# Output projection, feed-forward tail, embedding gate and second block's first products by tiles of tokens, and the recurrent input turned two chunks earlier

## The chip, the cores and the metric

The kernel runs on one core of a Trainium2 chip, in one launch. The metric is the time of that core in microseconds (us); less is better. TensorE (PE) multiplies, VectorE (DVE), ScalarE (ACT) and GpSimd (POOL) work on what it needs and leaves, and SyncE (SP) issues most of the transfers.

## The reference, cut to what matters

The program is two transformer blocks over 256 tokens of 1024 features, in fp32. Only the parts that the change touches are shown; the mixers' inside is left out.

```python
# first block
merged = sigmoid(ga) * (y_a @ w_branch_a) + sigmoid(gb) * (y_b @ w_branch_b)
h = x + rms_norm(merged @ w_out, norm_post_mix)
v = rms_norm(h, norm_pre_mlp)
h = h + rms_norm(square(relu(v @ w_up)) @ w_down, norm_post_mlp)
h = h + rms_norm((p @ w_ple) * sigmoid(h @ w_ple_gate), norm_ple)
# second block
u2 = rms_norm(h, g_mix)
qa, ka, va, qb, kb, vb, qi, ki, wi, ga, gb = split(u2 @ w_in_2)
qa, ka = rope(qa), rope(ka)
...
x = x + hier_moe(...)   # 32 experts: 188 MB of weights, read at the program's end
```

## The kernel before

**Tiling.** The 256 tokens lie in two tiles `tt` of 128. `h` holds tokens on the partitions, while a product needs features there, so `h` is turned by PE transposes (`tps`) wherever it enters a product. Every fp32 operand is a pair, a rounded high part and a low part that is the rest, and every product is three passes (high by high, low by high, high by low). A weight matrix comes in chunks of 1 MB, 1024 rows by 256 columns. `wchunk` fetches one on SP's queue into `wraw` (3 buffers), then ACT casts it to `whi` in two halves (line 254) and DVE subtracts to give `wlo` in two halves (line 256), each with 2 buffers. A chunk is 48 matmuls of 256 columns. `fm` gives features on the partitions, both tiles of tokens in one matmul; `tm` and `tms` give tokens on the partitions, one tile after the other.

**Stages around the change.** In `mixer`, four chunks of `w_branch_b` on the attention's output (`mbb`), then the recurrent output `hg` is turned into `ya` (`tsplit`, 16 transposes) and four chunks of `w_branch_a` (`mba`) are multiplied with it and merged into `mh`. `w_out` (`mo`) takes two chunks for both tiles and the last two tile by tile. `PostNorm` then does, for each tile, a square with a running sum on ACT (`pm_j`, line 406), a multiply by the gain on DVE (`pm_fo`, line 407), a chain of nine small DVE operations for the inverse root (lines 198 to 214), and the update of `h` in two halves (line 414). `Turn.do(tt)` turns one tile of `h`: 8 transposes into two PSUM banks, and for each bank, if a gain goes in, a DVE multiply to `gx` (line 328), an ACT cast (line 329) and a DVE subtract (line 330), all of 128x512; without a gain an ACT cast and a DVE subtract (lines 362, 363). `products` are 48 matmuls on the embedding (`mple`) that depend on none of this. `feed_forward` goes over 16 chunks up (`mup`, relu squared on DVE, POOL, ACT, DVE into `hid`) and 16 down (`acc`, 512 columns, 24 matmuls a chunk); the last two chunks down go together, tile 0 first. Then PostNorm `pf`, the turn `pg`, the gate's product (`mpg`, four chunks in two pairs, each pair tile 0 then tile 1), PostNorm `pp`, the turn `u2`, and `block2`: `mmaq` in two chunks by tile, `mmak` in two chunks, ropes on DVE and POOL, transposes `px`, the index key `pxki`.

**What sets the order.** Each engine runs its instructions in one fixed order. A scheduler builds the order at compile time from the code's order, priorities and its own estimates, except where `tc.manual_schedule` pins PE to the code's order. `issue_after` keeps an instruction behind a named one on its engine. An operation early in an engine's order that still waits holds up all behind it.

Of the kernel before, what the change touches and what calls it, by code (L numbers as in the profile page):

```python
# [19 lines left out]
T = 256  # L20
# [12 lines left out]
T8 = 11  # L33
UNITS = 21
# [56 lines left out]
def tile_kernel(ctx: ExitStack, tc: tile.TileContext, a: dict, out: bass.AP, stages="1234", dbg=None):  # L91
# [92 lines left out]
    def rsqrt_steps(ss, dim, name, r, n=1, part=None):  # L184


        t = lambda k, dt=F32: small.tile([128, n], dt, name=name + k, tag="rn_" + k, bufs=4)
# [29 lines left out]
    def rsqrt_mean(ss, dim, name, out=None, n=1):  # L217
        r = out if out is not None else small.tile([128, n], F32, name=name + "r", tag="rn_r", bufs=4)
        run(rsqrt_steps(ss, dim, name, r, n))
        return r  # L220
# [16 lines left out]
    def wchunk(src, na, halves=False, after=None, act=None):  # L237
# [12 lines left out]
        hi = ws.tile([128, 2048], F32R, name="whi", tag="whi", bufs=2)  # L250
        lo = ws.tile([128, 2048], F32R, name="wlo", tag="wlo", bufs=2)
        for c in (slice(0, 1024), slice(1024, 2048)):
            with tc.issue_after(act) if act and c.start else ExitStack():
                cnt["hi"] = ACT.copy(hi[:, c], raw[:, c]).ins  # L254
            with tc.issue_after(after) if after else ExitStack():
                DVE.tensor_tensor(lo[:, c], raw[:, c], hi[:, c].bitcast(F32), op=OP.subtract)  # L256
# [91 lines left out]
    class Turn:  # L348
# [5 lines left out]
        def do(self, tt):  # L354
            hi, lo = self.u
            for k in (0, 4):
# [8 lines left out]
                self.end = scaled_split(hi[:, k:k + 4, c], lo[:, k:k + 4, c], ps, self.g[:, k:k + 4])  # L365

    def row_rstd(name, after=None):

        r = small.tile([128, 2], F32, name=name + "_r", tag="rr", bufs=4)
        for tt in range(2):  # L370
            ss = small.tile([128, 1], F32, name=name + "_ss", tag="rss", bufs=4)
            with tc.issue_after(after) if after and tt else ExitStack():
                ACT.activation(t8([128, D], name + "_j"), h[:, tt, :], AF.Square, accum_out=ss)
            rsqrt_mean(ss, D, name, r[:, tt:tt + 1])
        return r
# [151 lines left out]
    def embed():  # L527

        ptok = t8([128, 2, 256], "ptok")
        ACT.dma_start(ptok, a["p"][0, 0].rearrange("(c p) d -> p c d", p=128))  # L530
        px = t8([128, 2, T], "pxh", F32R), t8([128, 2, T], "pxl", F32R)
# [3 lines left out]
        def products():  # L535
            wp = wchunk(a["w_ple"][0].rearrange("(k p) c -> p k c", p=128), 2)
# [8 lines left out]
    def mixer():  # L545
# [384 lines left out]
        wb = a["w_branch_b"]  # L930
        for i in range(4):
            ps = mmt([128, 2, T], "mbb")
# [6 lines left out]
        ya = split2("ya")  # L939
        tsplit(hg, 8, *ya, g=gncol.to_broadcast([128, 8]))  # L940
        mh = split2("mh")
        for i in range(4):
            ps = mmt([128, 2, T], "mba")
# [849 lines left out]
```

## Time and profile before

| | us |
|---|---|
| median of 3 runs (lowest to highest) | 1313.97 (1312.89 to 1314.04) |
| the profiled execution's own time | 1311.6 |
| its span, first to last instruction | 1309.8 |
| PE busy | 1174.4 (90%) |
| DVE busy | 660.1 (50%) |
| ACT busy | 423.7 (32%) |
| POOL busy | 101.7 (8%) |

The profile is of one execution. Its time and its span differ by 1.8 us, which lie around the program. Where PE is busy in nearly every slice of a stage, each microsecond in which it stands still is a microsecond of that stage; late in the program the transfers of the experts' weights take all of the DMA engines. The views used further down are the page, tables of windows (busy time and count of instructions of each engine in a stretch, with PE's granted clock and the DMA share), the list of PE's waits, the rows of one engine in order of time, and groups of instructions by line.

### The profile page before, as it was taken

The page shows a single profiled execution, that of the slowest core. Times are in us where ns is not written, and L with a number is a line of the kernel's source. Part 1 is how long each engine was busy: PE and PEld are TensorE (multiplying, and loading weights), DVE is VectorE, ACT ScalarE, POOL GpSimd, SP SyncE. Part 2 cuts the span into 40 slices and gives each one's busy share as a digit, 9 for nine tenths or more (in the row PEclk, how much of TensorE's full clock was granted, in tenths as well). Part 3 has the DMA queues.
Part 4 walks back from the last instruction along what each step waited for, and adds up shares of the span by engine and source line. Part 5 has one row for each costly group of instructions (what it writes and reads, how often), then busy time and mean ns, then how long its engine had stood idle before and what let it go on. Part 6 is the DMA issues. An engine that isn't in the chain of part 4 may idle for free. (4 is left out here: it accounts for less than half of the span.)

```text
span 1309.8 us, 20713 instructions
## 1 busy us (share of the span) xinstructions
PE 1174.4 (90%) x8530; PEld 888.1 (68%) x8530; DVE 660.1 (50%) x1320; ACT 423.7 (32%) x799; POOL 101.7 (8%) x118
## 2 busy tenths in 40 slices
PE   7999999999998999998899999998969786877855
PEld 7898898999998999988798899963313222222211
DVE  6558876786667556657869776741101010101103
ACT  4455555244345434444444454420000000000001
POOL 0000000642001000010131011000000000000000
PEclk9999999999999999999899999999999899999998
DMA  8743433228564555564375474979999999999996
GB/s 265 258 132 103 129 108 118 66 66 189 172 205 136 186 179 184 191 201 152 91 236 173 160 265 163 368 296 426 427 426 428 427 426 427 426 427 427 427 423 236
DMA packets 145925, 332.15 MB, mean 254 GB/s; under 512 B 9169, under 2 KB 110498, under 8 KB 122274
## 3 DMA queue, kind: packets, MB, share of 16 engines
q1 hardware_dynamic: 140640, 327.18, 67.1%
q10 hardware_dynamic: 5186, 3.60, 1.0%
q8 instruction: 69, 1.13, 0.4%
q14 instruction: 30, 0.25, 0.1%
HBM read 329.70 MB, written 1.05 MB: 253 GB/s over the span
## 5 line engine op out<-in xcount | busy, mean ns | idle before, releaser
L256 DVE TENSOR_TENSOR wlo<-wraw,whi 128x1024 fp32r<-128x1024 f32 x226 | 292.7, 1314 | 107.4 <-ACT whi L254 107.4
L254 ACT CAST whi<-wraw 128x1024 fp32r<-128x1024 f32 x226 | 231.5, 1049 | 274.3 <-issue 64.7
L1518 PE MATMUL mh<-ew,xg 128*32 128x512 f32 x1024 | 184.9, 657 | 68.8 <-DMA ew<-in_w_dram 68.2
L1518 PEld LDWEIGHTS mh<-ew,xg 128*32 128x32 f32 x1024 | 42.4, 119 | 196.0 <-DMA ew<-in_w_dram 123.3
L1518 PE MATMUL ey<-ew,eth 128*32 128x512 f32 (+1 forms) x544 | 101.4, 572 | 14.9 <-DMA ew<-in_w_dram 14.3
L1518 PEld LDWEIGHTS ey<-ew,eth 128*32 128x32 f32 x544 | 26.8, 109 | 83.1 <-issue 40.8
L1000 PE MATMUL acc<-whi,hid 128*128 128x512 f32 x256 | 80.8, 395 | 0.7 <-DVE hid L989 0.7
L320 PE MATMUL mup<-v_hi,whi 128*128 128x256 f32 x256 | 72.5, 284 | 1.7 <-ACT v_hi L329 1.7
L320 PE MATMUL mgate<-u_hi,whi 128*128 128x256 f32 x256 | 73.2, 286 | 0.0
L1542 DVE SCALAR_TENSOR_TENSOR eth<-eth,gs,mh 128x512 f32<-128x512 f32 x8 | 6.0, 746 | 132.9 <-PE mh L1518 132.9
L320 PE MATMUL mup<-v_lo,whi 128*128 128x256 f32 x256 | 72.8, 284 | 0.1
L320 PE MATMUL mup<-v_hi,wlo 128*128 128x256 f32 x256 | 72.7, 284 | 0.0
L320 PE MATMUL mgate<-u_lo,whi 128*128 128x256 f32 x256 | 72.2, 282 | 0.0
L320 PE MATMUL mgate<-u_hi,wlo 128*128 128x256 f32 x256 | 72.1, 282 | 0.0
L1576 DVE TENSOR_TENSOR eyl<-ey,eyh 128x512 fp32r<-128x512 f32 (+1 forms) x17 | 11.1, 655 | 109.3 <-ACT eyh L1575 109.3
L1541 DVE SCALAR_TENSOR_TENSOR eth<-eth,mh 128x512 f32<-128x512 f32 x8 | 5.5, 687 | 104.2 <-ACT eth L1540 104.2
L1000 PEld LDWEIGHTS acc<-whi,hid 128*128 128x128 f32 x256 | 47.1, 188 | 12.1 <-DVE hid L989 1.5
L1548 ACT COPY eth<-ehT 128x512 f32<-128x512 f32 x8 | 4.7, 586 | 151.5 <-PE ehT L1547 151.5
L1000 PE MATMUL acc<-wlo,hid 128*128 128x512 f32 x128 | 50.9, 398 | 0.0
L320 PEld LDWEIGHTS mup<-v_hi,whi 128*128 128x128 f32 x256 | 48.9, 191 | 2.6 <-ACT v_hi L329 2.0
L320 PEld LDWEIGHTS mup<-v_lo,whi 128*128 128x128 f32 x256 | 49.0, 191 | 0.9 <-DVE v_lo L330 0.3
L320 PEld LDWEIGHTS mgate<-u_hi,whi 128*128 128x128 f32 x256 | 48.2, 188 | 1.6 <-issue 1.5
(661 smaller groups left out, 2833.3 us busy)
## 6 DMA issues: line engine op xcount, KB each, us to landing
ew<-in_w_dram SPq DMA_DIRECT2D x188, 1024.0 KB, 19.6
wraw<-in_w_in_dram SPq DMA_DIRECT2D x55, 1024.0 KB, 5.3
wraw<-in_w_up_dram SPq DMA_DIRECT2D x16, 1024.0 KB, 5.3
wraw<-in_w_down_dram SPq DMA_DIRECT2D x16, 1024.0 KB, 4.9
wraw<-in_w_out_dram SPq DMA_DIRECT2D x8, 1024.0 KB, 5.2
wraw<-in_w_branch_b_dram SPq DMA_DIRECT2D x16, 256.0 KB, 5.5
wraw<-in_w_branch_a_dram SPq DMA_DIRECT2D x4, 1024.0 KB, 5.1
wraw<-in_w_ple_gate_dram SPq DMA_DIRECT2D x4, 1024.0 KB, 5.2
```

The costliest lines, as they stand in the source:

```text
L254: cnt["hi"] = ACT.copy(hi[:, c], raw[:, c]).ins
L256: DVE.tensor_tensor(lo[:, c], raw[:, c], hi[:, c].bitcast(F32), op=OP.subtract)
L320: PE.matmul(ps[:, f, :], lhsT=w[v][:, k, c0 + f * 128:c0 + f * 128 + 128], rhs=x[u][:, k, :], start=k == 0 and i == 0, stop=k == nk - 1 an ...
L1000: PE.matmul(acc[tt][c], lhsT=x[:, p_, k, tt * 128:tt * 128 + 128], rhs=w[q_][:, k, c * 512:c * 512 + 512], start=j == 0 and k == 0 and i = ...
L1518: PE.matmul(ps[r, :], lhsT=lhsT[:, r], rhs=w[i][:, k, c], start=start, stop=stop)
L1541: DVE.scalar_tensor_tensor(hT, hT, 1.0, h1, op0=OP.add, op1=OP.mult)
L1542: DVE.scalar_tensor_tensor(hT, hT, gs, h3, op0=OP.mult, op1=OP.mult)
L1548: ACT.copy(hT, tp)
L1576: DVE.tensor_tensor(y[1], yp, y[0].bitcast(F32), op=OP.subtract)
```

## The change

- **Recurrent input.** `ya` is turned after the second of the four `mbb` chunks, with PE pinned to the code's order from there to the end of the first `up`. The last `mba` chunk is multiplied and merged in two halves.
- **Output projection.** The four `w_out` chunks are all kept, and tile 0 goes through all four (`quarter`: 24 matmuls of one tile and one chunk), then tile 1. The turn of tile 0 stands before tile 1's last quarter. `PostNorm` takes two pieces of 512 columns.
- **`Turn.do` with a gain.** Instead of three operations of 128x512 a bank, four slices of 128x128, each an ACT operation that scales and rounds from PSUM and a DVE operation that scales, subtracts and writes the low part. This holds for all turns with a gain: `u` at the start, `v`, and `u2`.
- **Feed-forward's tail.** Chunk 13 down moves behind chunks 14 and 15: tile 0 takes 13, 14, 15, then tile 1 takes 14, 15, 13, with the turn `pg` of tile 0 between 15 and 13.
- **Gate and second block.** The gate goes by quarters: tile 0 chunks 0 to 2, turn of tile 1, tile 0 chunk 3, tile 1 chunks 0 to 2, turn `u2` of tile 0, tile 1 chunk 3. `mmaq` and `mmak` become four chunks `mmaqk` in the same way, and the four ropes follow.
- **Weights.** `fifo` keeps the casts and subtracts of these chunks in issue order, and `room` puts some of them in extra buffers (`xhi`, `xlo`). `row_rstd` does both tiles in one chain.

SP's order of transfers, and the count of matmuls of each product, are the same in both.

```diff
@@ wchunk
+        hi = room([128, 2048], "xhi", F32R) if room else ws.tile([128, 2048], F32R, name="whi", tag="whi", bufs=2)
+        lo = room([128, 2048], "xlo", F32R) if room else ws.tile([128, 2048], F32R, name="wlo", tag="wlo", bufs=2)
         for c in (slice(0, 1024), slice(1024, 2048)):
-            with tc.issue_after(act) if act and c.start else ExitStack():
+            with tc.issue_after(cnt["hi"] if fifo else act) if fifo or act and c.start else ExitStack():
                 cnt["hi"] = ACT.copy(hi[:, c], raw[:, c]).ins
+            after = cnt["lo"] if fifo else after
...
@@ Turn.do
-                self.end = scaled_split(hi[:, k:k + 4, c], lo[:, k:k + 4, c], ps, self.g[:, k:k + 4])
+                for j in range(4):
+                    g = self.g[:, k + j:k + j + 1]
+                    cnt["split"] = ACT.activation(hi[:, k + j, c], ps[:, j, :], AF.Copy, scale=g).ins
+                    self.end = DVE.scalar_tensor_tensor(lo[:, k + j, c], ps[:, j, :], g, hi[:, k + j, c].bitcast(F32),
+                                                        op0=OP.mult, op1=OP.subtract).ins
@@ mixer
+        order = tc.manual_schedule(engines={PE.engine})
+        order.__enter__()
+        ya = split2("ya")
         for i in range(4):
+            if i == 2:
+                tsplit(hg, 8, *ya, g=gncol.to_broadcast([128, 8]))
...
+            w = wchunk(wcols(a["w_branch_a"][0], i * 256), 8)
+            for lo, hi in ((0, 2),) if i < 3 else ((0, 1), (1, 2)):
+                ps = mmt([128, hi - lo, T], "mba")
+                fm(ps, w, ya, c0=lo * 128, nf=hi - lo)
+                merge(ps, sga, sgb, mh, slice(2 * i + lo, 2 * i + hi))
...
+        w = [wchunk(wcols(a["w_out"][0], i * 256), 8, fifo=True, room=t8 if i in (0, 3) else None)
+             for i in range(4)]
         for tt in range(2):
+            for i in range(4):
+                if i % 2 == 0:
+                    ps = mmt([128, 2, 256], "mo")
+                if tt and i == 3:
+                    turn.do(0)
+                quarter(ps[:, i % 2, :], w[i], mh, tt)
+                if i % 2:
+                    pn.piece(i // 2, tt, ps.rearrange("p z c -> p (z c)"), 512)
+            pn.finish(tt, 2)
+    def quarter(ps, w, x, tt):
+        for k in range(8):
+            for i, (u, v) in enumerate(PASSES):
+                PE.matmul(ps, lhsT=x[u][:, k, tt * 128:tt * 128 + 128], rhs=w[v][:, k, :],
+                          start=k == 0 and i == 0, stop=k == 7 and i == 2)
@@ feed_forward
+        for j, w_ in tail:
+            down(0, j, w_, hid[j], last=j == 15)
+        finish(0)
+        w += [gate_w(i) for i in (1, 2)]
+        for j, w_ in tail[1:] + tail[:1]:
+            if j == 13:
+                turn.do(0)
+            down(1, j, w_, hid[j], last=j == 13)
+        finish(1)
...
+        for i in range(3):
+            gated(0, i)
+        turn.do(1)
+        w.append(gate_w(3))
+        gated(0, 3)
+        for i in range(4):
+            if i == 3:
+                then.do(0)
+            gated(1, i)
@@ block2
-        qw = [(mmt([128, 2, T], "mmaq"), wchunk(wcols(w_in, i * 256), 8, after=turn.end, act=cnt["split"] if i else None)) for i in range(2)]
-        tms(qw, u, mid=lambda: turn.do(1))
+        for i in range(3):
+            w.append(qk_w(i))
+            quarter(ps[i][:, 0], w[i], u, 0)
+        turn.do(1)
+        w.append(qk_w(3))
+        quarter(ps[3][:, 0], w[3], u, 0)
+        for i in range(4):
+            quarter(ps[i][:, 1], w[i], u, 1)
```

**Tail of the feed-forward, DVE.** `wlo` are the low parts of the gate's first two chunks, `pg_lo` the low part of the turned `h`, `pf_fo` and the `pf` operations PostNorm's. Before, from the update of tile 0 to the update of tile 1:

```order
L414 SCALAR_TENSOR_TENSOR h_76<-pf_fo_6280,pfr_6292,h_76 128x512 x2
L407 TENSOR_TENSOR pf_fo_6280<-acc10_4714,pf_g_6278 128x512
L363 TENSOR_TENSOR pg_lo_6283<-tps_6308,pg_hi_6282 128x4x128
L363 TENSOR_TENSOR pg_lo_6283<-tps_6315,pg_hi_6282 128x4x128
L407 TENSOR_TENSOR pf_fo_6280<-acc11_4715,pf_g_6278 128x512
L411 TENSOR_REDUCE pf_s2_6328<-pf_ss_6281 128x1
L256 TENSOR_TENSOR wlo_6355<-wraw_6352,whi_6354 128x1024
L198 TENSOR_SCALAR pfb_6331<-pf_s2_6328 128x1
L256 TENSOR_TENSOR wlo_6355<-wraw_6352,whi_6354 128x1024
```

In the changed kernel, from the update of tile 0:

```order
L419 SCALAR_TENSOR_TENSOR h_76<-pf_fo_6217,pfr_6267,h_76 128x512 x2
L259 TENSOR_TENSOR wlo_6286<-wraw_6283,whi_6285 128x1024 x2
L259 TENSOR_TENSOR wlo_6294<-wraw_6291,whi_6293 128x1024 x2
L366 TENSOR_TENSOR pg_lo_6220<-tps_6323,pg_hi_6219 128x4x128
L366 TENSOR_TENSOR pg_lo_6220<-tps_6330,pg_hi_6219 128x4x128
L412 TENSOR_TENSOR pf_fo_6217<-acc10_4734,pf_g_6215 128x512
L412 TENSOR_TENSOR pf_fo_6217<-acc11_4735,pf_g_6215 128x512
L416 TENSOR_REDUCE pf_s2_6355<-pf_ss_6218 128x1
L199 TENSOR_SCALAR pfb_6358<-pf_s2_6355 128x1
```

The four subtracts of the gate's weights now stand together between the first update of `h` and `pg_lo`, and no longer inside the chain of the second tile (before, two more followed there).

**Turn of `u2` for tile 0, ACT.** `pth` is the gate's tanh, `pp_j` PostNorm's square, and the casts are of the second block's first chunks. Before:

```order
L1027 ACTIVATE pth_6646<-mpg1_6491 128x512
L329 CAST u2_hi_4692<-gx_6633 128x4x128
L329 CAST u2_hi_4692<-gx_6642 128x4x128
L406 ACTIVATE pp_j_6649,pp_ss_6349<-pth_6646 128x512
L254 CAST whi_6715<-wraw_6713 128x1024
L373 ACTIVATE u2_j_6837,u2_ss_6836<-h_76 128x1024
L114 DMA cst2_6701<-in_cst_dram 128x384
L329 CAST u2_hi_4692<-gx_6774 128x4x128
L329 CAST u2_hi_4692<-gx_6783 128x4x128
```

In the changed kernel:

```order
L370 ACTIVATE u2_hi_4704<-tps_6607,colv_86 128x128
L256 CAST xhi_6720<-wraw_6718 128x1024
L370 ACTIVATE u2_hi_4704<-tps_6607,colv_86 128x128
L370 ACTIVATE u2_hi_4704<-tps_6620,colv_86 128x128
L256 CAST xhi_6720<-wraw_6718 128x1024
L256 CAST whi_6752<-wraw_6750 128x1024
L370 ACTIVATE u2_hi_4704<-tps_6607,colv_86 128x128
L370 ACTIVATE u2_hi_4704<-tps_6620,colv_86 128x128
L1069 ACTIVATE pth_6657<-mpg_6582 128x512
L256 CAST whi_6752<-wraw_6750 128x1024
L370 ACTIVATE u2_hi_4704<-tps_6607,colv_86 128x128
L370 ACTIVATE u2_hi_4704<-tps_6620,colv_86 128x128
```

The two casts of the turn have become eight slices; casts of the next weights, the last tanh and the last square stand between them.

**Second tile of the output projection, DVE.** `v_lo` are slices of tile 0's turn, `wlo_4740` the first `up` chunk. Before:

```order
L330 TENSOR_TENSOR v_lo_4567<-gx_4594,v_hi_4566 128x4x128
L330 TENSOR_TENSOR v_lo_4567<-gx_4603,v_hi_4566 128x4x128
L407 TENSOR_TENSOR pm_fo_4312<-mo1_4453,pm_g_4310 128x512
L411 TENSOR_REDUCE pm_s2_4610<-pm_ss_4313 128x1
L256 TENSOR_TENSOR wlo_4720<-wraw_4717,whi_4719 128x1024
L198 TENSOR_SCALAR pmb_4613<-pm_s2_4610 128x1
```

In the changed kernel:

```order
L412 TENSOR_TENSOR pm_fo_4323<-mo_4544,pm_g_4321 128x512
L371 SCALAR_TENSOR_TENSOR v_lo_4337<-tps_4569,colv_86,v_hi_4336 128x128
L416 TENSOR_REDUCE pm_s2_4622<-pm_ss_4324 128x1
L259 TENSOR_TENSOR wlo_4740<-wraw_4737,whi_4739 128x1024
L371 SCALAR_TENSOR_TENSOR v_lo_4337<-tps_4582,colv_86,v_hi_4336 128x128
L199 TENSOR_SCALAR pmb_4625<-pm_s2_4622 128x1
L259 TENSOR_TENSOR wlo_4740<-wraw_4737,whi_4739 128x1024
L371 SCALAR_TENSOR_TENSOR v_lo_4337<-tps_4582,colv_86,v_hi_4336 128x128
```

The second tile's chain had one subtract between `pm_fo` and `pmb`. Now it has a slice and a subtract before `pmb` and a slice, a subtract and a slice more behind it.

## Rows read from the trace of the kernel before

**Rows 1.** Page: span, engines with share and count, granted clock in 40 slices.

```profile
span 1309.8 us, 20713 instructions
...
PE 1174.4 (90%) x8530; PEld 888.1 (68%) x8530; DVE 660.1 (50%) x1320; ACT 423.7 (32%) x799; POOL 101.7 (8%) x118
...
PEclk9999999999999999999899999999999899999998
```

**Rows 2.** Windows at the end: length, each engine busy (count), clock, DMA share, GB/s.

```profile
860.00:870.00 10.00, 8.79 (x74) 5.34 (x74) 5.01 (x30) 2.30 (x8) 0.00 (x0) 1.00 0.37 131
870.00:880.00 10.00, 10.00 (x93) 5.18 (x94) 1.23 (x4) 0.64 (x2) 0.00 (x0) 1.00 0.99 407
880.00:1300.00 420.00, 328.33 (x1813) 107.61 (x1806) 55.23 (x108) 24.51 (x51) 0.00 (x0) 0.96 1.00 419
```

**Rows 3.** Windows of PE alone: length, busy (count), clock, DMA share, GB/s.

```profile
344.00:354.00 10.00, 8.86 (x69) 1.00 0.33 107
400.00:415.00 15.00, 11.24 (x75) 0.89 0.54 184
593.00:610.00 17.00, 13.38 (x91) 0.90 0.48 155
610.00:622.00 12.00, 12.00 (x102) 1.00 0.57 175
622.00:642.00 20.00, 15.24 (x100) 0.83 0.31 89
656.00:670.00 14.00, 12.05 (x101) 1.00 0.86 290
```

**Rows 4.** Windows of all engines, two at a low granted clock.

```profile
410.00:415.00 5.00, 5.00 (x32) 5.00 (x32) 2.49 (x10) 0.00 (x0) 0.00 (x0) 0.66 0.52 163
630.00:635.00 5.00, 5.00 (x23) 5.00 (x24) 5.00 (x16) 0.00 (x0) 0.00 (x0) 0.50 0.53 163
```

**Rows 5.** PE waits from 342 to 670: sum in us, times, longest.

```profile
PE mmaq L309 <- ACT u_hi L329: 2.2, 2, 1.2
PE mpg L309 <- DVE pfb L198: 2.0, 1, 2.0
PE mmaq L309 <- DVE ppb L198: 1.9, 1, 1.9
PE mup L320 <- ACT v_hi L329: 1.7, 1, 1.7
PE tps L359 <- DVE h L414: 1.6, 1, 1.6
PE pxki L1117 <- POOL ki L488: 1.4, 1, 1.4
...
PE acc L1000 <- DVE hid L989: 0.7, 2, 0.5
```

**Rows 6.** DVE in time, feed-forward tail: start, length, operation.

```profile
591.89 1.42 DVE L414 SCALAR_TENSOR_TENSOR h<-pf_fo,pfr,h 128x512 f32<-128x512 f32 x2
...
596.58 1.22 DVE L256 TENSOR_TENSOR wlo<-wraw,whi 128x1024 fp32r<-128x1024 f32 x1
...
597.77 1.22 DVE L256 TENSOR_TENSOR wlo<-wraw,whi 128x1024 fp32r<-128x1024 f32 x1
```

**Rows 7.** ACT in time, the same place.

```profile
588.72 0.60 ACT L406 ACTIVATE pf_j<-acc 128x512 f32<-128x512 f32 x1 [0.48 <-PE acc L1000]
```

**Rows 8.** ACT groups by line: count, busy, mean ns of one.

```profile
L254 ACT CAST whi<-wraw 128x1024 fp32r<-128x1024 f32 x226 | 231.5, 1049 | 274.3 <-issue 64.7 <-PE mup L320 60.9 <-PE acc L1000 40.3
...
L449 ACT ACTIVATE ats_p<-ats_s,ats_mx 128x128 f32<-128x128 f32 x16 | 6.0, 373 | 17.1 <-PE atw_pt L465 8.5 <-DVE ats_mx L447 8.5
```

**Rows 9.** DVE group by line and shape: count, busy, mean ns.

```profile
L1135 DVE SCALAR_TENSOR_TENSOR score<-rl,wi,score 128x128 f32<-128x128 f32 x8 | 2.7, 343 | 0.0
```

**Rows 10.** PE in time, program start, with the wait before.

```profile
11.76 0.58 PE L309 MATMUL mkv<-wlo,u_hi 128*128 128x256 f32 x1 [1.39 <-DVE wlo L256]
```

**Rows 11.** POOL in time, one rope of the second block.

```profile
660.97 2.12 POOL L488 TENSOR_TENSOR tokmak<-rope2z,rope2w 128x512 f32<-128x512 f32 x1 [4.48 <-DVE rope2z L486]
```

More of the change, by code (lines that the diff above doesn't have):

```diff
@@ L184, in rsqrt_steps @@
     def rsqrt_steps(ss, dim, name, r, n=1, part=None):
[L187 removed]
+        t = lambda k, dt=F32: small.tile([128, n], dt, name=name + k, tag=f"rn{n}" + k, bufs=3 if n == 1 else 1)
         b, sh, y, q, y2 = t("b"), t("s", I32), t("y"), t("q"), t("z")
@@ L217, in rsqrt_mean @@
     def rsqrt_mean(ss, dim, name, out=None, n=1):
-        r = out if out is not None else small.tile([128, n], F32, name=name + "r", tag="rn_r", bufs=4)
+        r = out if out is not None else small.tile([128, n], F32, name=name + "r", tag="rn1r", bufs=4)
         run(rsqrt_steps(ss, dim, name, r, n))
@@ L968, in merge, with feed_forward @@
         DVE.tensor_tensor(mh[1][:, c], sga[:, c], mh[0][:, c].bitcast(F32), op=OP.subtract)
-    def feed_forward(pw, turn, then):
+    def feed_forward(pw, turn, then, order):
         turn.do(1)
@@ L980, in up @@
             ps = mmt([128, 2, T], "mup")
-            fm(ps, wchunk(wcols(a["w_up"][0], j * 256), 8), v)
+            fm(ps, wchunk(wcols(a["w_up"][0], j * 256), 8, fifo=j == 0, after=turn.end if j == 1 else None), v)
             if j == 0:
@@ L986, in up @@
             POOL.tensor_tensor(r, r, r, op=OP.mult)
-            x = t8([128, 2, 2, T], "hid", F32R)
+            if j % 2 == 0:
+                hid["room"] = t8([128, 2, 2, 2, T], "hid", F32R)
+            x = hid["room"][:, j % 2]
             ACT.copy(x[:, 0], r)
@@ L1043, in block2 @@
         u = turn.u
-        qw = [(mmt([128, 2, T], "mmaq"), wchunk(wcols(w_in, i * 256), 8, after=turn.end, act=cnt["split"] if i else None)) for i in range(2)]
-        tms(qw, u, mid=lambda: turn.do(1))
+        ps = [(mmt if i < 3 else pt)([128, 2, T], "mmaqk") for i in range(4)]
+        w = []
+        qk_w = lambda i: wchunk(wcols(w_in, i * 256), 8, fifo=True, room=t8 if i in (0, 3) else None)
+        for i in range(3):
[6 more added lines that the diff above has]
+            quarter(ps[i][:, 1], w[i], u, 1)
+        order.__exit__(None, None, None)
+        qw, kw = ps[:2], ps[2:]
         r = row_rstd("u2", after=cnt["split"])
@@ L1726, in tile_kernel @@
     if "1" in stages:
-        pw, turn = mixer()
+        pw, turn, order = mixer()
     else:
```

128 lines of the change are left out of this document (60 added, 68 removed).

## The prediction

> **What bounds the kernel now.** I read the page first. PE is busy for 90% of the span [rows 1], so the question is where it stands still and whether the end would follow if it didn't. The windows late in the program answer the second part: from 880 us to 1300 us the DMA engines are full (share 1.00, 419 GB/s), while in the ten microseconds up to 870 their share is 0.37 [rows 2]. The end is 420 us of transfers of expert weights that start once the computation ahead of them has released buffers. So time saved on PE before 870 us should move the start of that block, and with it the end, one for one. Time saved inside the block would be worth nothing, but the change touches nothing there.
>
> Next I read the windows of PE alone around the places of the change. A stretch in which PE runs full gives the measure: 102 matmuls in the 12 us from 610 [rows 3], 0.118 us each (matmuls of 256 columns; those of 512, as in the products down, count twice). Against that measure:
> - 344 to 354, the turn of the recurrent output: 69 matmuls are 8.1 us of work, so 1.9 are lost.
> - 400 to 415, end of the output projection and first product up: 75 are 8.8, so 6.2 are lost.
> - 593 to 610, turn for the gate: 91 are 10.7, so 6.3 are lost.
> - 622 to 642, turn for the second block: 100 are 11.8, so 8.2 are lost.
> - 656 to 670, ropes and index key: 101 are 11.9, so 2.1 are lost [rows 3].
>
> Together 24.7 us: that is the ceiling for these places. Seven items of the list of waits name 11.5 us of it [rows 5]. A good part of the rest is the clock: from 630 to 635 the granted clock is 0.50, which is 1.2 GHz instead of 2.4, and 23 matmuls fit where 42 would, a loss of 2.2 us; from 410 to 415 it is 0.66, 32 matmuls, a loss of 1.2 us [rows 4]. Both spells begin right behind a place where PE stood still.
>
> **The change part by part.** Prices used throughout: a cast of half a chunk on ACT 1.05 us [rows 8], a subtract of half a chunk on DVE 1.2 us [rows 6]. The trace has no slice of the new turn. The nearest rows are an ACT operation of 128x128 with a per-partition operand, 0.37 us [rows 8], and a DVE operation of the same kind and size, 0.34 us [rows 9]. The order of the changed kernel lets the ACT slice of a bank wait for the DVE slice before it in that bank, so I take 0.71 us for each of a bank's four steps, 2.9 us a turn. Bounds: 0.37 if the two overlap, 1.3 if a slice cost what operations four times as long do (0.60 on ACT and 0.71 on DVE for 128x512 [rows 6, 7]).
>
> The Trainium skill, page PSUM — Partial Sum Buffer, section "PSUM bank collisions raise a hardware error", says that ACT and DVE must not be in one bank at once and that the compiler therefore makes one wait for the other, reads included. This rule speaks against cutting a bank into slices. No row of before shows it. Without it the turn would go at ACT's 0.37 us a step, and the term of the output projection below would be better by about 1 us.
>
> *Start.* The first pass on a low part waits 1.39 us for a subtract [rows 10]. The turn at the start also goes by slices, so DVE no longer does two whole multiplies and two whole subtracts ahead of it. Gain 0.8, between -0.3 (the slices hold up the casts of the weights) and 1.3 (all of the wait).
>
> *Recurrent input.* The transposes, casts and subtracts of `ya` now lie under 96 matmuls of the last two `mbb` chunks, 11.3 us of PE. DVE has four subtracts (4.8 us), two products and the turn (about 5.5 us) in them, so they fit, just. The wait for `ya` goes. Gain 1.8 of the 1.9, between 1.0 and 1.9.
>
> *Output projection.* Tile 0's chain and turn now lie under tile 1's quarters (24 matmuls, 2.8 us each), and cost nothing. Tile 1's don't: behind the last `mo` matmul, PE has 48 matmuls of the embedding, 5.65 us. The chain then needs the square, which stands behind casts on ACT (0.75 late, then 0.8 with its read), two subtracts and three slices that the order puts inside it (2.4 + 1.0), the small operations (1.25) and the update (1.4): 7.6 us. So PE still waits about 1.9 us at the transposes, where it waits 1.6 now [rows 5]. Then the first product up takes slices as they come: first low part after 0.71, the next only 1.05 us later still, because the square of the next norm stands on ACT between the first two slices; then one each 0.71 against 0.35 us of matmuls. That is 2.5 us of waiting, against 1.7 for the wait at that place now [rows 5]. Half speed behind it again, more likely than not: 0.7 of 1.2. Together 5.1 us lost, where 6.2 are lost now, and 0.2 more (of the 0.7 for `hid` [rows 5]) at the first product down. Gain 1.3, between -0.5 and 3.5.
>
> *Feed-forward's tail.* Tile 0's chain takes 4.6 us from the square of its last piece (588.72) to the end of the update (593.31) [rows 6, 7]. Now 24 matmuls of 512 columns of tile 1 lie over it, 5.6 us. The transposes then need not wait. Then come 12 matmuls of chunk 13, 2.8 us, and 0.9 of transposes. DVE does four subtracts (4.8 us) and the first `pg_lo` (0.7) after the update, 5.5 us, so `mpg` waits for about 0.6. I add 0.6 for the third gate chunk's weights, and 0.4 for small things. Tile 1's chain lies under 72 matmuls (8.5 us) and is free. The stop of 2.0 us for a subtract [rows 5], which stands in the order between the chain's operations, goes, and with it the half speed. Loss 1.6 instead of 6.8 (6.3, and ahead of the window 0.5, the longest wait for `hid` [rows 5]). Gain 5.2, between 3.5 and 6.5.
>
> *Gate to second block.* Tile 0's chain is covered by 72 matmuls in the same way. But the turn `u2` has only 24 matmuls, 2.8 us, over it, and on ACT casts stand between its slices. Counted from the end of the transposes along the order: five slices and three casts take 4.7 us, the tanh 0.6, a cast 1.0, so the fourth slice of the first bank is done at 6.6 and PE needs it at 3.9; a square and another cast stand before the last slice, done at 9.1. Ideally the first quarter ends at 5.6; by this it ends at 9.8. So 4.2 us lost, or about 1.5 if the casts run earlier than this order lets me see, and 0.4 for a chance of half speed behind it. Tile 1's chain and turn lie under the quarters and are free. Loss 4.4 instead of 8.2. Gain 3.8, between 0.5 and 6.5.
>
> *Ropes.* Four ropes of 2.1 us each on POOL [rows 11] now come one behind the other after one norm of both tiles, where they were spread over the products; the last transposes wait for them. Loss 0.4, between -1.0 (a gain, from the doubled chain) and 1.5. The wait for the index key, 1.4 [rows 5], stays. SP's transfers keep their order.
>
> Sum: 0.8 + 1.8 + 1.3 + 5.2 + 3.8 - 0.4 = 12.5 us. The profiled execution took 1311.6 us, 2.4 less than the median of 1313.97. Taken off the profile that gives 1299.1, off the median 1301.5.
>
> **The rivals.** *All cover holds.* If the slices overlap and casts don't stand in their way, the output projection loses 2.5 and the second block 1.5, and no half speed is left: 12.5 + 2.6 + 2.9, and the upper ends of start and tail (0.5 + 1.3), make 20 us, 1294. For it: PE has matmuls enough that don't depend on the turns. Against it: the order itself, in which ACT waits at slices with casts queued behind.
>
> *The waits come back.* ACT and DVE are in order, and every slice that waits holds casts, and every cast a product. If the second block's loss stays at 8 and the output projection's at 6.7, only the start, the recurrent input and 4 us of the tail are left, less 0.4: 6 us, 1308. For it: the wait of 2.0 us at the gate [rows 5] was of just this kind, a subtract behind a small operation that waited. Against it: 7 us of that loss are waits and clock which the quarters cover by counts.
>
> *Slower.* One mechanism: each step from ACT to DVE and back in one bank costs more than the two operations. Four turns lie open or nearly so (both at the start, the second `v`, the first `u2`), 16 steps; at 0.8 us more a step, 1.5 instead of 0.71, the gain is gone, and at 1.8, 1.1 more, the kernel is at 1319. Against it: now the chain from the square to the update, with its handings over, takes 4.6 us in all [rows 6, 7].
>
> *The end does not follow.* If the transfers of the expert weights were paced by something that the change doesn't move, the windows up to 870 us would show less waiting and the time would stay at 1313. For it: SP's order is unchanged. Against it: the share of 0.37 just before the block [rows 2]; the transfers wait for the computation there, not the other way round.
>
> **How the numbers follow.** Forecast of 1301.5, 0.58; all cover holds 0.14; the waits come back 0.17; the end does not follow 0.06; slower 0.05. A measurement of this kernel can tell about 0.2%, 2.6 us, from no change. Faster by more: the first three, less a little of the third, 0.87. Within: 0.09. Slower: 0.04. The range reaches from the first rival's 1294 to a little beyond the second's 1308, 1293.5 to 1309, with about 0.2 left out: the two last cases and tails of the first.
>
> **What the changed kernel's profile would show.** Right: no wait of PE at `mba`; transposes of `pg` and of tile 0's `v` without one; granted clock near full around the gate; waits left at the second `v` turn (1.9, then 2.5) and at the first `mmaqk` for `u2` (about 4); the DMA block beginning near 867 instead of 880. Wrong: a low granted clock at three places as before; waits for `xlo` or `wlo` in the gate's quarters of over 1 us; waits at `hid` or at the extra buffers, which share their room with it; a DMA block that begins no earlier.

## The result, and the profile after

The changed kernel takes 1296.09 us (median; 1293.66 to 1296.35) where the kernel before took 1313.43 beside it: 17.3 us less, ratio 0.9865 (95% interval 0.9847 to 0.9882). On another chip it took 1295.90 against 1312.33, 16.4 us less, ratio 0.9875 (0.9860 to 0.9890). The forecast was 12.5 us less, 1301.5 in a range of 1293.5 to 1309.0.

The page of the changed kernel, its span, engines and granted clock, beside [rows 1]:

```profile
span 1294.3 us, 20749 instructions
...
PE 1172.1 (91%) x8530; PEld 883.9 (68%) x8530; DVE 658.2 (51%) x1327; ACT 429.7 (33%) x832; POOL 100.0 (8%) x118
...
PEclk9999999999999999999999999999989899999988
```

The span is 15.5 us shorter and PE's busy time 2.3: most of the gain is time in which PE stood idle before. The medians differ by 1.8 us more than the spans, since the profiled execution of before (1311.6) was that much faster than the median of its runs, while the one of after (1296.05) was at its median.

Windows of PE alone at the places of the change (length, busy with count, clock, DMA share, GB/s), to be held against [rows 3]:

```profile
344.00:354.00 10.00, 10.00 (x87) 1.00 0.75 242
398.00:413.00 15.00, 13.38 (x99) 1.00 0.43 142
594.00:610.00 16.00, 15.62 (x131) 1.00 0.33 105
614.00:630.00 16.00, 14.35 (x101) 0.89 0.72 221
640.00:656.00 16.00, 14.05 (x118) 1.00 0.60 187
```

At 0.118 us a matmul, nothing is lost where `ya` is turned (87 matmuls in 10 us, 69 before), 3.3 us in the 15 us around the first product up (99, and 75 before), 0.5 us over the gate, 4.1 us in 614 to 630, the turn of `u2`, and 2.1 us in 640 to 656, the ropes. PE's waits between 330 and 657 us (sum, times, longest), beside [rows 5]:

```profile
PE pxki L1179 <- POOL ki L493: 1.5, 1, 1.5
PE tps L362 <- DVE h L419: 1.3, 1, 1.3
PE mmaqk L979 <- ACT u_hi L370: 1.0, 1, 1.0
PE mmaqk L979 <- DVE u_lo L371: 0.5, 1, 0.5
```

The stops at `mba`, and the long ones for a subtract at the gate (2.0 us) and in the second block (1.9), have gone. What is left of 1 us or more is the wait for the update at `tps`, the one for the slices of `u2`, and the one for the index key (1.4 before). The end followed: in the window below the DMA engines are full, and by windows of 2 us they are nearly so (0.94) from 855 us on, where before they were (0.90) from 870 on.

```profile
857.00:867.00 10.00, 10.00 (x93) 5.87 (x86) 1.47 (x3) 0.60 (x1) 0.00 (x0) 1.00 1.02 427
```

From the views by tile I read where the first or last matmul of each product starts, and so how much earlier than before each stage ends. Each column is the gain of one stretch in us (negative is a loss); each kernel's are of its one profiled execution.

| kernel | start to first `mbb` | to first `mo` | to first `acc` | to last `mpg` | to `pxki` | to the last matmul |
|---|---|---|---|---|---|---|
| the changed kernel | -0.10 | 2.37 | 2.33 | 4.76 | 5.89 | 0.31 |
| x12_changed_again (the same) | 0.19 | 2.37 | 2.40 | 4.74 | 5.53 | -0.54 |
| x9_u2_chain_first | 0.74 | 2.37 | 2.41 | 4.76 | 8.80 | 0.39 |
| x10_tail_by_chunks | -1.73 | 2.11 | 2.42 | -2.95 | 6.02 | 0.12 |
| x11_all_first | 0.68 | 2.11 | 4.09 | 4.76 | 8.82 | 0.36 |
| x6_u2_slices_first | 1.81 | 2.12 | 2.35 | 5.38 | 7.30 | -0.42 |
| x7_v_and_u2_first | 0.87 | 2.37 | 2.90 | 4.61 | 5.80 | -1.40 |
| x1_whole_turns | -3.14 | 1.99 | 2.85 | 5.50 | 5.04 | -0.50 |
| x2_ya_alone | -2.28 | 2.12 | -0.23 | 0.17 | -0.22 | -0.16 |
| x3_out_by_chunks | 1.15 | 2.12 | 1.75 | 5.25 | 6.01 | 0.48 |
| x4_tail_gate_by_chunks | 0.62 | 2.38 | 2.40 | -0.11 | 1.45 | 0.11 |
| x5_qk_by_chunks | 1.89 | 2.38 | 2.30 | 5.38 | 2.41 | 0.49 |
| x8_first_turn_cut | -0.36 | -0.22 | -0.71 | 0.0 | 0.0 | 0.18 |

In the changed kernel the eight transposes of the first `u2` lie ahead of the last `mpg` and no longer behind it (0.87 us), so by equal work tail and gate gained 5.6 and the second block 5.0. After `pxki` the gain stays as it is to the end.

### The profile page after: what moved, and what is told of

It reads as the page before. It is cut to its first block, busy times and chain, and to the rows that moved or that the text cites. A ratio compares the mean times of both kernels' runs of the same rounds, so it can differ in the third digit from the quotient of the medians.

```text
span 1294.3 us, 20749 instructions
## 1 busy us (share of the span) xinstructions
PE 1172.1 (91%) x8530; PEld 883.9 (68%) x8530; DVE 658.2 (51%) x1327; ACT 429.7 (33%) x832; POOL 100.0 (8%) x118
## 5 line engine op out<-in xcount | busy, mean ns | idle before, releaser
L259 DVE TENSOR_TENSOR wlo<-wraw,whi 128x1024 fp32r<-128x1024 f32 x210 | 272.5, 1315 | 92.0 <-ACT whi L256 91.8
L256 ACT CAST whi<-wraw 128x1024 fp32r<-128x1024 f32 x210 | 215.6, 1051 | 237.3 <-PE mup L323 55.0
L1580 PE MATMUL mh<-ew,xg 128*32 128x512 f32 x1024 | 187.7, 669 | 66.9 <-DMA ew<-in_w_dram 66.8
L1019 PE MATMUL acc<-whi,hid 128*128 128x512 f32 x240 | 75.3, 394 | 0.2 <-DVE hid L1009 0.2
L1019 PEld LDWEIGHTS acc<-whi,hid 128*128 128x128 f32 x240 | 44.3, 188 | 10.5 <-DVE hid L1009 0.5
L1637 ACT CAST eyh<-ey 128x512 fp32r<-128x512 f32 (+1 forms) x17 | 9.5, 561 | 120.6 <-PE ey L1580 113.8
```

Of the source, the lines that this page charges most:

```text
L259: cnt["lo"] = DVE.tensor_tensor(lo[:, c], raw[:, c], hi[:, c].bitcast(F32), op=OP.subtract).ins
L1019: PE.matmul(acc[tt][c], lhsT=x[:, p_, k, tt * 128:tt * 128 + 128], rhs=w[q_][:, k, c * 512:c * 512 + 512], start=first and k == 0 and i == ...
L1580: PE.matmul(ps[r, :], lhsT=lhsT[:, r], rhs=w[i][:, k, c], start=start, stop=stop)
L1637: ACT.copy(y[0], yp)
```

## The experiments

The theory: each place gave what PE's waits and the low clock behind them cost there, the gains add up, and what the changed kernel still loses is order on ACT and DVE. Twelve kernels ran; the table above has a row for each. One thing no run takes apart: each that takes back the order by tiles also takes back `fifo` and the extra buffers of that place, so what those give by themselves is not shown.

**Recurrent input alone.** The kernel before, with PE in the code's order from the gates to the last `mba`, and:

```diff
         for i in range(4):
+            if i == 2:
+                tsplit(hg, 8, *ya, g=gncol.to_broadcast([128, 8]))
             ps = mmt([128, 2, T], "mbb")
```

> The kernel before with one edit: the recurrent input turned two chunks earlier, PE in the code's order from there to the last mba. Theory: the wait of 0.7 and 0.25 us at mba and the slow matmuls behind go, 2.3 us faster than before, 1311.1. Rival (DVE is full there, and the wait moves to wlo of the next chunks, or the time is given back at the transposes further on): within 0.5 us of before, 1313.

Measured: 1310.11 against 1311.49, ratio 0.9981 (0.9968 to 0.9993), 2.5 us by the ratio. In the trace the stretch is 2.1 us shorter, and in every kernel with the edit 2.0 to 2.4. The theory holds; the rival's 0.5 us lies just outside of the interval, which begins at 0.9.

**First turn alone.** The kernel before with slices in the turn `u`.

```diff
+                if self.cut:
+                    for j in range(4):
+                        g = self.g[:, k + j:k + j + 1]
+                        cnt["split"] = ACT.activation(hi[:, k + j, c], ps[:, j, :], AF.Copy, scale=g).ins
...
-        turn = Turn("u", gain["norm_pre_mix"])
+        turn = Turn("u", gain["norm_pre_mix"], cut=True)
```

> The kernel before with one edit: the first turn of all, u, cut into slices. The changed kernel is 1.67 us ahead at 60 us, but level with before at 270 us. Theory A (the two places where it was given back, a low granted clock near 97 us and a collision of DVE and POOL near 257 us, follow from the earlier start): ahead by 1.7 us at 60 us, level at 320 us, 1313. Theory B (they are chance, and not tied to the start): ahead by 1.7 us at 320 us too, 1311.7.

Measured: 1310.29 against 1311.49, ratio 0.9990 (0.9980 to 1.0001): 1.3 us by the ratio, unclear. The profiled execution was 1.67 us ahead at 42 us and 0.4 behind at the first `mbb`, as theory A says, but the times say no such thing, and the early part turned out to differ between executions of the same code: with nothing changed up to 320 us, the kernel with `ya` alone came to its first `mbb` 2.3 us later than the kernel before. So neither theory can be told from one trace. Read together, the traces bear out theory A for the low clock near 97 us, and show what goes with the rest of the spread (last section).

**Whole turns.** The changed kernel with `scaled_split` for `u`, `v` and `u2` again.

```diff
-                for j in range(4):
-                    g = self.g[:, k + j:k + j + 1]
...
+                self.end = scaled_split(hi[:, k:k + 4, c], lo[:, k:k + 4, c], ps, self.g[:, k:k + 4])
```

> The changed kernel with the turns u, v and u2 in whole operations of 128x512 again (DVE multiply, ACT cast, DVE subtract). Theory (a step of ACT and DVE in one bank takes 0.79 us, so slices cost little and bring the first part of a turn sooner): 1.7 us lost at the start and 1 to 2 at the turns of v and u2, 1297 to 1299. Rival (whole operations put fewer instructions between ACT's casts, and the waits at u2 and v get shorter): 1 to 3 us faster, 1293 to 1295.

Measured: 1298.07 against 1311.49, ratio 0.9898 (0.9865 to 0.9930). The interval takes in the changed kernel. By stretches, from the first `mbb` on, whole turns gain 0.5 at the output projection and 0.7 over the tail and lose 0.4 at the recurrent input, 0.9 at the second block and 0.8 behind it: 0.8 in all. The other 3.0 us that it is behind the changed kernel lie ahead of `mbb`, where executions of the same code differ as much, so they can't be put down to the edit. The slices may be worth about 1 us by the stretches and 3 by the ratios, but a gain of theirs is not shown.

**Output projection by chunks.** The changed kernel with the old code from `PostNorm("pm")` to `products`.

```diff
+        order.__exit__(None, None, None)
...
-            for i in range(4):
-                if i % 2 == 0:
-                    ps = mmt([128, 2, 256], "mo")
-                if tt and i == 3:
-                    turn.do(0)
-                quarter(ps[:, i % 2, :], w[i], mh, tt)
...
+            pn.piece(1, tt, po[tt].rearrange("p z c -> p (z c)"), 512, 2)
+            pn.finish(tt, 3)
+            if tt == 0:
+                turn.do(0)
```

> The changed kernel with the output projection, the embedding's products and the first up chunk as before (by chunks, PE's order left to the scheduler); all else changed. Theory (the places add up, and this part gave the 2.3 us by which PE gained between the last mba and the first acc): 2.3 us slower than the changed kernel, 1298.4, with waits of about 1.6 and 1.7 us at tps and mup and a low granted clock behind them. Rival (the gain there came from the slices of the turn, which stay): within 0.5 us of the changed kernel.

Measured: 1296.39 against 1311.96, ratio 0.9890 (0.9874 to 0.9907). In the stretch, 1.75 of the 2.33 us stay. The longest of its waits there:

```profile
PE tps L362 <- DVE h L419: 2.2, 1, 2.2
```

The wait for the update is longer, and the granted clock is 0.74 from 400 to 405 us, but no wait is listed at the first product up. So the slices without the order by tiles keep 1.75 us here; the order by tiles without the slices, in the run above, kept 2.85. Either alone gives most of what both give, and in the trace the rival is nearer; the time does not settle it.

**Tail and gate by chunks.** The changed kernel with the old end of `feed_forward`, from the last products down to the gate.

```diff
+        down([14, 15])
...
-        for i in range(3):
-            gated(0, i)
-        turn.do(1)
-        w.append(gate_w(3))
-        gated(0, 3)
+        for i in (0, 2):
...
+            tms(items, turn.u, mid=None if i else lambda: turn.do(1))
```

> The changed kernel with the last chunks down and the gate as before (chunks 14 and 15 last, the gate in two pairs of chunks); all else changed. Theory (the tail and the gate by tiles gave 4.8 us): about 4.8 us slower than the changed kernel, 1301, with the wait of 2 us and the low granted clock behind the turn for the gate. Rival (part of that comes back because PE's next stop is shorter): 2 us slower, 1298.

Measured: 1304.55 against 1311.49, ratio 0.9944 (0.9923 to 0.9965). Tail and gate lose all their 4.8 us, and the second block 4.4 of its 5.9 as well (5.7 and 3.6 by equal work, since the transposes of `u2` lie behind the last `mpg` again):

```profile
PE mpg L312 <- DVE pfb L199: 2.0, 1, 2.0
PE mmaqk L979 <- DVE u_lo L371: 1.8, 2, 0.9
PE mmaqk L979 <- ACT xhi L256: 1.4, 1, 1.4
PE mmaqk L979 <- DVE xlo L259: 1.0, 1, 1.0
```

The old wait of 2.0 us is back, and with the gate by chunks nothing lies over the turn `u2`: PE waits for casts, subtracts and slices of `mmaqk`. I had not expected that. So the gate's quarters serve the next stage too.

**Tail alone by chunks.** The changed kernel with chunks 13 to 15 down in the old order and the gate by quarters.

```diff
-TAIL = 3
+TAIL = 2
...
+        for j, w_ in tail:
+            down(1, j, w_, hid[j], last=j == 15)
         finish(0)
         w += [gate_w(i) for i in (1, 2)]
-        for j, w_ in tail[1:] + tail[:1]:
-            if j == 13:
-                turn.do(0)
-            down(1, j, w_, hid[j], last=j == 13)
+        turn.do(0)
         finish(1)
```

> The changed kernel with the feed-forward's last three chunks down in the old order (13 for both tiles, then 14 and 15 by tile, then both updates), the gate by quarters. With tail and gate both old, 4.9 us were lost at the gate and 4.4 at the second block. Theory (the 4.9 us belong to the tail, the 4.4 to the gate's quarters, which put work over the turn u2): 4 to 5 us slower than the changed kernel, all of it between the last up and the end of the gate; the second block as in the changed kernel; 1300.5. Rival (the tail's order matters only with the gate old): within 1 us of the changed kernel.

Measured: 1303.89 against 1312.33, ratio 0.9932 (0.9919 to 0.9945). The second block keeps its gain, as the theory says. The tail loses 7.7 us, more than it had gained. The waits of the gate's first products for the turned `h`, 0.5 us and less in the changed kernel, are 3.5 together, and the one for `hid` is longer than in either kernel. The clock adds to it, granted at 0.78 from 585 to 590 us and at 0.74 from 595 to 600:

```profile
PE mpg L979 <- DVE pg_lo L366: 2.0, 1, 2.0
PE acc L1019 <- DVE hid L1009: 1.7, 1, 1.7
PE mpg L979 <- ACT pg_hi L365: 1.5, 1, 1.5
```

**Second block by chunks.** The changed kernel with `mmaq` and `mmak` as before.

```diff
-        for i in range(3):
-            w.append(qk_w(i))
-            quarter(ps[i][:, 0], w[i], u, 0)
-        turn.do(1)
...
+        tms(qw, u, mid=lambda: turn.do(1))
```

> The changed kernel with the second block's first chunks as before (two chunks mmaq by tile, then two chunks mmak); all else changed, the gate by quarters and the turn in slices too. Theory (the quarters of mmaqk gave the 5.9 us): about 6 us slower than the changed kernel, 1302, with a low granted clock and waits behind the turn u2 as before. Rival (the slices and the gate's quarters gave most of it): about 2 us slower, 1298.

Measured: 1298.31 against 1311.96, ratio 0.9908 (0.9891 to 0.9925). 3.5 us of the stretch are lost, between theory and rival: 2.4 stay, 1.5 by equal work. Without the gate's quarters (and with the tail in the old order) 1.4 stayed, with both kinds of quarters 5.0: each needs the other. PE's longest wait here is for a subtract, and the clock behind it is 0.66 from 615 to 620 us:

```profile
PE mmaq L312 <- DVE wlo L259: 3.3, 1, 3.3
```

**Slices ahead of casts at `u2`.** The changed kernel with the first chunk's casts ahead of the turn and everything else on ACT behind its last slice.

```diff
             if i == 3:
-                then.do(0)
-            gated(1, i)
+                qk0 = then.first()
+                with tc.issue_after(cnt["hi"]):
+                    then.do(0)
+                with tc.issue_after(cnt["split"]):
+                    gated(1, i)
+                continue
```

> The changed kernel, but the casts of the second block's first chunk go ahead of the turn u2 of tile 0 on ACT, and the casts of the next chunk and the last tanh go behind its eight slices. Theory (the 4.4 us lost in the first 72 matmuls of mmaqk are casts standing between slices, and the low clock behind is their consequence): the waits of 0.95 and 0.54 go, no granted clock under 0.95 between 615 and 625 us, the end is 3 to 4 us earlier, about 1292.5. Rival (the clock falls at this place anyway, or ACT's casts then come too late for the second chunk): the waits move to wlo of the next chunk, at most 1.5 us earlier, about 1295.

Measured: 1294.82 against 1311.96, ratio 0.9877 (0.9860 to 0.9895), as the changed kernel. The waits for slices have gone, as the theory says, and a new one has come, which neither theory nor rival had:

```profile
PE tps L362 <- DVE h L419: 2.4, 1, 2.4
```

DVE in order of time ahead of that update (start, length, operation):

```profile
617.20 0.15 DVE L416 TENSOR_REDUCE pp_s<-pp_ss 128x1 f32<-128x2 f32 x1
617.27 1.21 DVE L259 TENSOR_TENSOR wlo<-wraw,whi 128x1024 fp32r<-128x1024 f32 x1
...
618.46 1.21 DVE L259 TENSOR_TENSOR wlo<-wraw,whi 128x1024 fp32r<-128x1024 f32 x1
...
619.66 1.21 DVE L259 TENSOR_TENSOR xlo<-wraw,xhi 128x1024 fp32r<-128x1024 f32 x1
...
620.85 1.21 DVE L259 TENSOR_TENSOR xlo<-wraw,xhi 128x1024 fp32r<-128x1024 f32 x1
...
622.87 0.16 DVE L215 SCALAR_TENSOR_TENSOR ppr<-ppq,ppz 128x1 f32<-128x1 f32 x1
623.07 1.42 DVE L419 SCALAR_TENSOR_TENSOR h<-pp_fo,ppr,h 128x512 f32<-128x512 f32 x2
```

Between the first and the last of the small operations stand four subtracts of 1.2 us. It is the pattern of [rows 6] again, one place further on.

**The same at `v`.** The same edit at the output projection, the first `up` chunk's subtracts behind tile 1's update, and the square behind the last slice.

```diff
                 if tt and i == 3:
-                    turn.do(0)
+                    wp = weights()
+                    with tc.issue_after(cnt["hi"]):
+                        turn.do(0)
...
+            if j == 0:
+                cnt["hi"], cnt["lo"] = cnt["sq"], cnt["h"]
...
-                Rb.append(row_bcast(row_rstd("v"), "v")[:, None, :].to_broadcast([128, 2, T]))
+                Rb.append(row_bcast(row_rstd("v", after=cnt["split"]), "v")[:, None, :].to_broadcast([128, 2, T]))
```

> As the run before, and the same at the output projection: the embedding's weights are cast ahead of the turn v of tile 0, the first up chunk's low parts come behind tile 1's update of h on DVE, and the square of the next norm behind the last slice of tile 1's turn on ACT. Theory (what is left there is order: two subtracts and slices inside the chain, a square between the slices): the wait of 1.3 us at the transposes goes, and the first product up loses about 1 us less of its 2.0; with the run before about 6 us off the changed kernel, 1290. Rival (the subtracts then come too late and the wait moves to the first product up): no more than 0.5 us better than the run before.

Measured: 1295.52 against 1311.96, ratio 0.9874 (0.9858 to 0.9891). The wait at the transposes has gone, and the stretch gains 0.6 us on the changed kernel, which is the rival's number. But it is not the rival's reason: no wait for `wlo` has come, and what takes the gain back is the granted clock, 0.90 and 0.76 in the ten us from 400. In `x11_all_first`, whose code is the same up to there and whose waits at the first product up are the same 0.54 and 0.20 us, the clock stays at 1.00, PE does 67 matmuls in these ten us and not 56, and the stretch gains 1.75 on the changed kernel, near the theory's 2.3. The time is no better than the run before; in the profiled execution a second spell of low clock lies in the second block (last section).

**Chain ahead of subtracts.** To the two runs before, one line (and in the first of them the name `cnt["h"]` for the update, which the second has):

```diff
+        cnt["lo"] = cnt["h"]
         w.append(qk_w(3))
```

It moves the fourth chunk's two subtracts (`xlo`) behind the update; the other two stay inside the chain.

> As x6_u2_slices_first, and the two subtracts of the fourth mmaqk chunk go behind tile 1's update of h on DVE. In x6 the transposes of u2 for tile 1 waited 2.4 us for that update, with five subtracts standing inside its chain. Theory (a subtract inside a chain of small operations delays it by its whole 1.2 us): that wait falls to about 0.3 us, PE loses 2 us less, and the time is 1.5 to 2 us under x6, about 1293. Rival (the wait moves to the fourth chunk's low part): no change, 1294.8.

> As x7_v_and_u2_first, with the same edit as the run before. Theory: the output projection gains 0.5 us against the changed kernel as in x7, the second block 3.5 us, 1292.5. Rival: as the changed kernel, 1296.

Measured, beside the changed kernel on the same chip (1295.90): with the edit at `u2` alone 1292.92, ratio to before 0.9858 (0.9842 to 0.9874); with both places 1290.80, ratio 0.9839 (0.9825 to 0.9854). The wait of 2.4 us is 0.4, and from 585 to 660 us no low clock is left in either. The line of waits, and the windows of all engines with the edit at `u2` alone:

```profile
PE tps L362 <- DVE h L419: 0.4, 1, 0.4
```

```profile
614.00:620.00 6.00, 6.00 (x52) 6.00 (x52) 5.32 (x10) 6.00 (x10) 0.00 (x0) 1.00 0.23 55
620.00:625.00 5.00, 4.43 (x34) 3.78 (x33) 4.75 (x12) 2.69 (x5) 0.00 (x0) 1.00 0.81 250
625.00:630.00 5.00, 4.95 (x41) 4.95 (x42) 3.75 (x11) 2.91 (x8) 0.00 (x0) 1.00 0.67 206
```

The second block now gains 8.8 us instead of 5.9. The kernel with all of it is 5.1 us faster than the changed one, and its interval lies below that one's; with the edit at `u2` alone it is 3.0 us, and the intervals overlap. So `x11_all_first` did better than its theory said (1292.5), in good part since the output projection gave 1.75 us and not the 0.5 that I had taken over from the run with the low clock.

> The changed kernel itself, for a comparison on one chip and for a second trace. If the early part differs by chance from run to run, the stretch from 228 to 323 us will differ by up to 3 us from the first trace, and the stretches of the change by less than 0.5.

This run gave the second time of the first section. Its stretches of the change differ from the first trace by 0.4 us at most. The stretch from 228 to 323 us was level with the first, so a spread between executions of one kernel is not shown; it shows between kernels whose code there is the same.

## Why the prediction was right

Direction and mechanism held, and the time lies in the range; the gain was 4 to 5 us larger than forecast. In the traces, which the sum was made from, it was 15.25 us against 12.5; the rest is the profiled execution of before, faster than its median. By its number the time is nearer to the rival "all cover holds" (1294) than to the forecast (1301.5), but not by that rival's reasons: the slices of a bank did not overlap, PE still waited for slices at `u2`, and the clock fell there. Step by step:

- **The end follows.** Right: 15.25 us earlier at `pxki`, 15.56 at the last matmul. The block of transfers began near 855 us and not near 867: the prediction took 880 for its start in the kernel before, where [rows 2] have the DMA engines full from 870.
- **Start**, 0.8 forecast: 0.7 to 2.1 us ahead at 42 us in the kernels with slices (1.0 in the one without), anything from 0.2 behind to 1.3 ahead at 100 us; by the times of the first turn alone 1.3, not certain. At the first `mbb` 0.1 behind in the trace of the changed kernel: nothing of this term is in the 15.25.
- **Recurrent input**, 1.8 forecast, 1.9 at most: 2.4, and 2.1 alone. The bound was the loss of one window of 10 us; the stretch is longer.
- **Output projection**, 1.3 forecast: 2.3. The waits came where they were put, but smaller: 1.3 us at the transposes (1.9 forecast), and 2.0 more in the window from 398, nearly all in the first product up (2.5). The steps of a bank went as the rows had said, 0.79 us from slice to slice (0.71 taken). The term for half speed, 0.7, was wrong: the clock stayed at 1.00.

```profile
404.89 0.61 ACT L370 ACTIVATE v_hi<-tps,colv 128x128 fp32r<-128x128 f32 x2
405.68 0.62 ACT L370 ACTIVATE v_hi<-tps,colv 128x128 fp32r<-128x128 f32 x2 [0.17 <-DVE v_lo L371]
406.47 0.69 ACT L370 ACTIVATE v_hi<-tps,colv 128x128 fp32r<-128x128 f32 x2 [0.16 <-DVE v_lo L371]
```

and DVE beside it:

```profile
405.30 0.60 DVE L371 SCALAR_TENSOR_TENSOR v_lo<-tps,colv,v_hi 128x128 fp32r<-128x128 f32 x2
...
406.08 0.35 DVE L371 SCALAR_TENSOR_TENSOR v_lo<-tps,colv,v_hi 128x128 fp32r<-128x128 f32 x1
...
406.42 0.34 DVE L371 SCALAR_TENSOR_TENSOR v_lo<-tps,colv,v_hi 128x128 fp32r<-128x128 f32 x1
```

- **Tail**, 5.2 forecast: 5.6.
- **Gate to second block and ropes**, 3.8 - 0.4 forecast: 5.0. This is the term that was furthest off. The windows of before that I summed stop at 642 and start again at 656; in 642 to 650 another 0.7 us were lost, which the sum leaves out. And the ropes cost nothing more: their place lost 2.1 before and 2.1 after. The loss that stays was nearly right, 4.1 against 4.4 (the two terms named for it make 4.2 + 0.4 = 4.6; how 1.5 was weighed against 4.2 is not said), but that is luck, for its make-up was another: the fourth slice was done 5.7 us behind the transposes and not 6.6, the last 7.8 and not 9.1, so PE waited 1.5 us for slices; then the clock fell (0.74 in 620 to 625: 34 matmuls, 1.0 us lost), which I had priced at 0.4:

```profile
615.49 0.64 ACT L370 ACTIVATE u_hi<-tps,colv 128x128 fp32r<-128x128 f32 x2
615.99 0.62 ACT L1069 ACTIVATE pth<-mpg 128x512 f32<-128x512 f32 x1
616.47 1.08 ACT L256 CAST whi<-wraw 128x1024 fp32r<-128x1024 f32 x1
617.41 0.67 ACT L370 ACTIVATE u_hi<-tps,colv 128x128 fp32r<-128x128 f32 x2
617.92 0.68 ACT L411 ACTIVATE pp_j<-pth 128x512 f32<-128x512 f32 x1
...
618.53 1.09 ACT L256 CAST whi<-wraw 128x1024 fp32r<-128x1024 f32 x1
...
619.47 0.42 ACT L370 ACTIVATE u_hi<-tps,colv 128x128 fp32r<-128x128 f32 x1
```

PE's own windows there, with 34 matmuls in 5 us where 42 fit:

```profile
615.00:620.00 5.00, 3.35 (x19) 0.92 0.55 172
620.00:625.00 5.00, 5.00 (x34) 0.74 0.72 193
```

and the window of before that the sum leaves out:

```profile
642.00:650.00 8.00, 7.46 (x62) 1.00 0.08 13
```

- **The rival "the waits come back"** decided nothing here, but the kernels by chunks show that it was real: with the tail and the gate by chunks it took back 3.6 us, by equal work, at the second block. **"Slower"** was out: a step cost 0.79, not 1.5.
- On the Trainium skill's rule (page PSUM — Partial Sum Buffer, section "PSUM bank collisions raise a hardware error"): the trace agrees. ACT's slices at 405.68 waited 0.17 us for DVE's slices of 405.30, and so on down the turn. What such a step costs, 0.79 us, only the rows tell.

## What to carry to other kernels

Splitting a stage by tiles pays at the stage behind it: it leaves independent products to lie over the next turn, so undoing one stage's tiles can cost several us one stage further on (3.6 here). When the order of an engine is free, look for a long operation inside a chain of short ones and for casts between the slices that PE waits for. Where PE waits for the end of such a chain, each can cost its whole length: two subtracts of 1.2 us moved behind it took 2.0 us off the wait. Moving one can uncover the next (2.4 us uncovered, then 5.1 us gained in all). Sum the losses over one unbroken stretch, not over the windows that look bad.

## What the runs showed of the hardware

**The clock doesn't fall at every stop.** Two kernels have the same stop of 2.38 us at the same transposes and the same work around it. In one the granted clock stays at 1.00, in the other it is 0.66 over the next 5 us (30 matmuls, where 44 fit): 1.5 us. Windows of PE alone, without the edit at `v` and with it:

```profile
619.00:624.00 5.00, 2.62 (x22) 1.00 0.81 257
625.00:630.00 5.00, 5.00 (x44) 1.00 0.97 353
```

```profile
620.00:625.00 5.00, 2.62 (x23) 1.00 0.81 255
625.00:630.00 5.00, 4.99 (x30) 0.66 1.09 384
```

A closer pair are the two kernels with the edit at `v`, whose code is the same up to there: behind the same waits in the first product up the clock is 0.76 from 405 to 410 us in `x7_v_and_u2_first` and 1.00 in `x11_all_first` (35 and 43 matmuls). So a stop by itself does not settle whether half speed follows, and the terms for it in the sum should have been bounds; what settles it is not shown.

The early start can have a price of this kind: in the changed kernel the clock falls at 96 to 100 us, on work with no long stop of its own (29 matmuls, 41 before); in a kernel with the same code up to there, the output projection by chunks, it does not. The two come there at other times, 1.7 and 0.8 us ahead of the kernel before. All six traces that are 1.6 us or more ahead at 94 us have a clock of 0.60 to 0.68 there and lose 0.4 to 0.9 us; of the seven others, one has a low clock (0.73, at 0.6 us ahead). That goes together; why is not shown.

```profile
92.00:96.00 4.00, 3.82 (x36) 1.00 0.56 167
96.00:100.00 4.00, 4.00 (x29) 0.62 0.30 99
```

```profile
92.00:96.00 4.00, 3.82 (x35) 1.00 0.29 76
96.00:100.00 4.00, 4.00 (x40) 1.00 0.55 190
```

**A DVE operation that takes 0.40 or 0.84 us.** In the recurrent mixer, 24 identical multiplies on DVE run beside multiplies on POOL. In the kernel before they take about 0.40 us until the one at 261.79, which takes 0.84; in the changed kernel the first long one is at 257.07 (0.89). Each moves the chain behind it. DVE groups of that line from 250 to 276 us (mean ns), before and in the kernel with `ya` alone, whose code is the same there:

```profile
L890 DVE TENSOR_TENSOR hq<-hq,hFp 128x256 f32<-128x256 f32 x24 | 13.1, 566 | 0.0
```

```profile
L890 DVE TENSOR_TENSOR hq<-hq,hFp 128x256 f32<-128x256 f32 x23 | 13.8, 621 | 0.0
```

POOL has the counterpart. In the kernel before, its multiply beside a short one of DVE takes 0.92 to 0.99 us between 254 and 261 us, and the first beside a long one, at 261.71, takes 0.63: where DVE's is short POOL's is long, and the other way round, as if one of the two waited for the other. Their starts do not tell which: POOL's leads by 0.06 us at 260.79, where DVE's is short, and by 0.05 at 257.02 in the changed kernel, where it is long. What decides it was not tried.

From 228 us to the first `mbb` the executions differ by up to 3.7 us on the same code, and the multiplies of over 0.7 us go with that. In the five traces where 11 of the 24 take that long (9 do in the kernel before) the stretch is 1.0 to 2.7 us longer than before, in the four with 6 to 8 it is 0.2 to 1.1 shorter. Another part is a low clock there in some (0.93 over 275 to 300 us with `ya` alone, 1.00 before).
